# A row block transposed by DMA instead of TensorE in a fused matrix product and RMS norm, and loads moved behind transposes

## The chip, the core and the metric

One core of one Trainium2 chip. The metric is device microseconds of one execution, as the median of three runs. A profiled execution has its own time, the program's span and a little around it.

## The reference

```python
x = np.matmul(a, b)                 # a, b: 2048 x 2048, float32
rms = np.sqrt(np.mean(x ** 2, axis=-1, keepdims=True) + eps)
return (gamma * x / rms).astype(np.float32)
```

## The kernel before

The 16 row blocks of `a` (128 rows each) are multiplied with `b`, which lies in SBUF as bf16 (`raw[j][kp]`, left or right half of the columns j, a pair of 128-row tiles kp). Two scratch memories matter: SBUF tiles and eight PSUM banks, `tbank` and `acc[0]` to `acc[6]`, each 128 x 512 f32. The schedule is manual: every engine works through its instructions in the order in which the code lists them, and semaphores order the engines against each other. An engine that waits holds back all that is listed behind it on the same engine. The same is true of POOL's and SP's DMA issues.

**Head (blocks 0 to 3).** While `b` streams in, TensorE transposes these blocks into `head_at` and forms their left half plainly, then the right half of blocks 0 and 1 plainly (`stream_right`, banks `plain` = `acc[0]` to `acc[3]`). The right half of blocks 2 and 3 (`PAIR`) goes by a seven-product scheme (Strassen-Winograd): two blocks by two halves of K, and sums of quarters of `a` and of `b` in place of an eighth product. Its banks are `u2` = `acc[4]`, `u4` = `acc[5]`, `p7` = `acc[6]`. `b_diff` and `b_rest` build the sums of `b` on DVE.

**Groups (blocks 4 to 15).** Group g holds blocks 2g and 2g+1, g = 2 to 7; a half n is a group and a column half j. `do(n, m)` issues product m of half n, eight matmuls of 128 x 128 by 128 x 512, into its bank, and for m = 1, 6, 7 an ACT copy of that bank. `take(n, ..)` brings a result chunk from PSUM to its x tile on ACT or adds it on DVE. `a_sums(g, which)` builds on DVE the sums of quarters of `a` that products 3, 5, 6 and 7 load as weights: sum 2 for product 6, sum 3 for product 7, sum 4 for product 3; product 5 uses sum 1. Groups 4 and 5, and 6 and 7, share a second level of the scheme (`step`, `b_two`, `a_two_sums`, `block_segment`, `last_group`).

**A block's way in.** `load_block(mb)` puts a 1 MB load on POOL's DMA queue; the tile comes from a pool of two, except block 8's, which lies in the second half of `head_flat`. `wait_for(x)` is a one-element copy on POOL, which holds every later load until x is there. `row_norm(mb)` is two squares and a root on ACT, `row_factor` four tiny DVE operations that make a power of two, and DVE scales the block to fp16. Blocks 6 and later go through `prepare`: two scaled halves (`a16_half` and the block's own memory), each transposed by a DMA on SP's queue (`dma_start_transpose`) into `at_even` or `at_odd`. Blocks 4 and 5 are scaled whole (`row_apply`, lines 244 to 246) and transposed on TensorE (`transpose_half`, line 198), eight 128 x 128 transposes per half, into `tbank` and another bank, and copied from there (`take_transposed`, line 205).

**A block's way out.** `square_half` and `square_right` (ACT) sum the squares and take the root, `take_pre` adds parts on DVE, `finish(mb, ..)` takes the reciprocal and scales each half on DVE and stores it from SP. A slot of `x_slot` serves several blocks, so a later `take` waits for the store before.

Around the change the order before is, at the top level (lines 519 to 558): the pair's product 7, product 6 into `u2`, the DVE copy `u4` <- `u2` (line 529), scaling of blocks 4 and 5, product 3 into `acc[0]`, product 5 into `u4`, the transposes of block 4, product 4 into `u2` with the two halves of block 5's transposes (`turn`) inside and behind it, `load_block(8)`, and block 5's sums. Then `first_segment` runs half 0, and `segment(n)` the rest. Inside `segment(n)`, product 3 of the half before and product 1 of the half behind are listed among the half's own. Half n = 0 runs 1, 7, 2, 6, half 1's product 1, then 5 and 4.

Of the kernel before, what the change touches and what calls it, by code (L numbers as in the profile page):

```python
# [17 lines left out]
def kernel(  # L18
# [13 lines left out]
    nc = tc.nc  # L32
# [215 lines left out]
    def prepare(mb):  # L248
        row_factor(mb)
        src, f = a32.pop(mb), factor.pop(mb)  # L250
        for h, dst in enumerate((a16_half, src.bitcast(FP16)[:, 0:HALF])):
            nc.vector.tensor_scalar_mul(out=dst, in0=src[:, h * HALF:(h + 1) * HALF], scalar1=f)
            nc.sync.dma_start_transpose(at(mb)[:, h * KP:(h + 1) * KP, :], dst)
# [222 lines left out]
    def stream_right(kp):  # L476
# [11 lines left out]
        if kp == KP - 1:  # L488
            product_matmul(PAIR, 1, 7, p7, kp - 1, True)
        product_matmul(PAIR, 1, 2, u4, kp, True)  # L490
# [4 lines left out]

    for kp in range(KP):
# [22 lines left out]
    r2, r3 = HB - 2, HB - 1  # L519
    x11, x12, x21, x22 = (x_chunk(r, c) for r in (r2, r3) for c in (2, 3))  # L520
    copy_on("A")(out=x11, in_=u2)
# [6 lines left out]
    product(PAIR, 1, 6, u2, start=False)  # L528
# [5 lines left out]
    row_apply(HB + 1)  # L534
    evict(plain[2:3], "A")
    product(PAIR, 1, 3, acc[0])
    product(PAIR, 1, 5, u4, start=False)
    turned = [transpose_half(HB, h, (tbank, acc[1])[h]) for h in range(2)]
    take_transposed(HB, 0, turned[0], nc.scalar.copy)
    take_transposed(HB, 1, turned[1], nc.vector.tensor_copy)  # L540
    load_block(HB + 3)
    for r in range(HB):
        take_pre(r)
    square_right(0)
    evict(plain[3:], "A")
    square_right(1)

    def turn(h):
        view = transpose_half(HB + 1, h, (tbank, acc[2])[h])
        take_transposed(HB + 1, h, view, nc.vector.tensor_copy)  # L550

    for kp in range(KP):
        if kp == 6:
            turn(0)
        product_matmul(PAIR, 1, 4, u2, kp, False)
    turn(1)
    load_block(HB + 4)
    a_sums(G0, (3, 1, 2), False)

    def pair_ends():  # L560
        nc.scalar.copy(out=x22, in_=p7)
        nc.scalar.copy(out=x12, in_=u4)
        add(x21, u2, x22)
        add(x22, x12, x22)
        add(x12, acc[0], x12)
# [4 lines left out]
    B1, B2, B3, B7 = (acc[1], acc[0]), acc[3:5], (acc[6], acc[5]), acc[2]  # L570

# [4 lines left out]
    def do(n, m, copies=True):  # L576
# [4 lines left out]
        b1, b2, b3 = B1[n % 2], B2[n % 2], B3[n % 2]  # L581
# [13 lines left out]
    def take(n, what, engine="A"):  # L595

        x11, x12, x21, x22 = chunks(n)
        if what == 11:
            copy_on(engine)(out=x11, in_=B1[n % 2])
# [11 lines left out]
    def first_segment():  # L611
        n, g, j = 0, G0, 0
        nxt = 2 * g + 2
        do(n, 1)
        do(n, 7, False)
        finish(0, (1,))
        pair_ends()
        do(n, 2)
        row_norm(nxt)
        a_sums(g, (4,))  # L620
        finish(0, (0,))
        do(n, 6)
        do(n + 1, 1)
        prepare(nxt)
# [287 lines left out]
```

## Time and profile before

| | |
|---|---|
| median of 3 runs | 219.05 us (219.04 to 219.17) |
| profiled execution | 218.97 us |
| its span | 217.2 us |
| granted TensorE clock | 0.995 |
| TensorE busy | 207.3 us, 95% |
| VectorE busy | 161.4 us, 74% |
| ScalarE busy | 113.1 us, 52% |
| GpSimd busy | 35.6 us, 16% |
| DMA moved | 46.60 MB, mean 215 GB/s |

Rows of the timeline give the start in us, the duration, the engine, the line, the operation with the tile written and read, and the shape; rows that follow each other are merged with a count. In brackets stands the idle time of that engine before the row and what ended it. A row "SPq" or "POOL DMA" is the issue of a DMA, not the transfer. Durations of neighbouring rows of one engine overlap a little, since they are pipelined.

### The profile page before, as it was taken

To read this page: it belongs to the slowest core of one execution; us is meant where nothing else is said; L and a number is where in the kernel's file an instruction comes from. 1 tells how busy PE (TensorE), PEld (TensorE's weight loads), DVE (VectorE), ACT (ScalarE), POOL (GpSimd) and SP (SyncE) were. 2 spreads that over 40 slices of the span, in tenths; PEclk is the share of its full clock that TensorE was granted. 3 is DMA by queue.
4 is the path that set the end of the run, shared out by engine and by line. 5 is a ranking of instruction groups with operands and counts; after the bars stand their busy time and mean duration, and the time that the engine had idled before them with its cause. 6 is when DMAs were issued, how large, how long until landed. Compare 5 with 4: busy or idle time off the path is not lost.

```text
span 217.2 us, 2953 instructions
## 1 busy us (share of the span) xinstructions
PE 207.3 (95%) x1000; PEld 97.2 (45%) x1020; DVE 161.4 (74%) x323; ACT 113.1 (52%) x222; POOL 35.6 (16%) x74
## 2 busy tenths in 40 slices
PE   7999999999999999999999999999999999999960
PEld 3544544444455444444444444444444444444420
DVE  1128869999899997788975899399859883385771
ACT  2110002900599569498626962585777651555771
POOL 7554444334001000100021001102010000000020
PEclk9999999999999999999999999999999999999997
DMA  7999999999959798978674975499985960040455
GB/s 152 168 202 210 201 204 210 212 206 213 405 202 382 290 263 229 330 295 241 162 239 172 340 246 96 187 237 271 278 307 153 284 218 0 0 193 3 193 191 195
DMA packets 37040, 46.60 MB, mean 215 GB/s; under 512 B 22561, under 2 KB 26657, under 8 KB 35745
## 3 DMA queue, kind: packets, MB, share of 16 engines
q0 software_dynamic: 10608, 23.86, 44.8%
q1 hardware_dynamic: 26144, 22.29, 33.9%
q10 hardware_dynamic: 272, 0.26, 0.3%
q8 instruction: 8, 0.13, 0.2%
q14 instruction: 8, 0.06, 0.1%
HBM read 34.60 MB, written 16.78 MB: 237 GB/s over the span
## 4 chain that ended last, share of the span: by engine, by line
PE 68%; DMA 23%; DVE 2%; POOL 2%; issue 2%; ACT 1%; ACTq 0%; DVEq 0%; POOLq 0%
PE acc L361 61%; DMA b<-in_b_dram 18%; DMA early<-in_a_dram 5%; PE acc L400 3%; PE tbank L400 2%; POOL b L115 1%; DVE early L101 1%; PE tbank L361 1%; POOL early L119 1%; ACT a L779 1%; PE acc L198 0%; PE tbank L198 0%; DVE acc L529 0%; DVE x L101 0%; DVE b L101 0%
## 5 line engine op out<-in xcount | busy, mean ns | idle before, releaser
L361 PEld LDWEIGHTS <-s 128*128 128x128 f16 (+1 forms) x312 | 30.5, 98 | 36.9 <-DVE s L338 0.3
L275 ACT ACTIVATE sq<-x 128x1024 bf16<-128x1024 f32 (+1 forms) x33 | 33.2, 1005 | 22.6 <-DVE x L101 18.8
L409 PE MATMUL acc<-b,head_at 128*128 128x512 bf16 x171 | 42.1, 379 | 0.2
L314 DVE SCALAR_TENSOR_TENSOR x<-x,r,gamma_sb 128x1024 f32<-128x1024 f32 x28 | 35.0, 1282 | 0.5
L361 PE MATMUL acc<-b,head_at 128*128 128x512 bf16 x135 | 33.9, 379 | 0.2
L101 DVE TENSOR_TENSOR x<-acc,x 128x512 f32<-128x512 f32 x33 | 22.2, 686 | 12.5 <-PE acc L361 6.7
L361 PEld LDWEIGHTS <-head_at 128*128 128x128 f16 (+1 forms) x192 | 18.7, 98 | 22.2
L361 PE MATMUL acc<-b,at_even 128*128 128x512 bf16 x110 | 26.2, 379 | 0.1
L361 PE MATMUL acc<-early,s 128*128 128x512 bf16 x100 | 25.3, 379 | 0.2
L409 PEld LDWEIGHTS <-head_at 128*128 128x128 bf16 x176 | 16.9, 98 | 19.1
L361 PE MATMUL acc<-b,s 128*128 128x512 bf16 x102 | 24.1, 379 | 0.2
L227 ACT ACTIVATE sq<-a 128x1024 bf16<-128x1024 f32 x22 | 23.3, 1058 | 1.7 <-DMA a<-in_a_dram 1.4
L361 PEld LDWEIGHTS <-at_even 128*128 128x128 f16 x160 | 15.6, 98 | 18.6
L361 PE MATMUL acc<-t_left,s 128*128 128x512 bf16 x93 | 22.2, 379 | 0.1
L115 POOL DMA_DIRECT2D b<-in_b_dram x32 | 17.2, 540 | 20.5 <-DMA b<-in_b_dram 13.8
L448 ACT COPY x<-acc 128x512 f32<-128x512 f32 x7 | 4.0, 581 | 25.3 <-PE acc L409 25.3
L591 ACT COPY acc<-acc 128x512 f32<-128x512 f32 x12 | 6.9, 575 | 10.4 <-PE acc L361 10.4
L190 DVE COPY head_at<-tbank 128x1024 bf16<-128x1024 bf16 x7 | 4.8, 693 | 7.5 <-PE tbank L185 7.5
L296 DVE RECIPROCAL r<-rms 128x1 f32<-128x1 f32 x16 | 2.5, 159 | 9.7 <-ACT rms L291 9.7
L101 DVE TENSOR_TENSOR x<-tbank,x 128x512 f32<-128x512 f32 x9 | 6.2, 690 | 4.2 <-PE tbank L438 4.1
L782 POOL TENSOR_SCALAR x<-x,r 128x512 f32<-128x512 f32 x2 | 1.4, 688 | 47.8 <-DVE r L296 47.8
L593 ACT COPY x<-acc 128x512 f32<-128x512 f32 x10 | 5.8, 584 | 5.3 <-PE acc L361 4.9
(129 smaller groups left out, 243.4 us busy)
## 6 DMA issues: line engine op xcount, KB each, us to landing
out_dram<-x SPq DMA_DIRECT2D x29, 512.0 KB, 3.0
a<-in_a_dram POOLq DMA_DIRECT2D x9, 1024.0 KB, 6.0
b<-in_b_dram POOLq DMA_DIRECT2D x32, 256.0 KB, 9.9
a<-in_a_dram POOLq DMA_DIRECT2D x4, 512.0 KB, 9.8
early<-in_a_dram POOLq DMA_DIRECT2D x7, 256.0 KB, 10.0
gamma_sb<-in_gamma_dram POOLq DMA_DIRECT2D x2, 512.0 KB, 9.8
head_at<-in_a_dram POOLq DMA_DIRECT2D x1, 1024.0 KB, 7.8
out_dram<-x SPq DMA_DIRECT2D x3, 256.0 KB, 2.6
```

Of the source, the lines that this page charges most:

```text
L101: nc.vector.tensor_tensor(out=out, in0=in0, in1=in1, op=op)
L115: nc.gpsimd.dma_start(out=raw[j][kp][:, t, :], in_=b[lo:lo + P, j * HALF:(j + 1) * HALF])
L190: nc.vector.tensor_copy(out=head_at[:, 2 * kp:2 * kp + 2, :, :], in_=view)
L227: nc.scalar.activation(out=junk, in_=a32[mb][:, h * HALF:(h + 1) * HALF], func=ACTF.Square, scale=2.0 ** -8, accum_out=n2[:, h:h + 1])
L275: nc.scalar.activation(out=sq[:, 0:src.shape[-1]], in_=src, func=ACTF.Square, scale=inv_sqrt_n, accum_out=msq[mb][:, c:c + 1])
L314: nc.vector.scalar_tensor_tensor(out=x, in0=x, scalar=inverse_of[mb], in1=gamma_sb[:, h * HALF:(h + 1) * HALF], op0=ALU.mult, op1=ALU.mult)
L361: nc.tensor.matmul(bank, lhsT[:, kp, :], rhs, start=(start and kp == 0), stop=(kp == KP - 1), skip_group_check=not start)
L400: nc.tensor.matmul(bank, lhsT[:, k, :], rhs, start=(m in (1, 7) and k == 0), stop=(k == KQ - 1), skip_group_check=m not in (1, 7))
L409: nc.tensor.matmul(bank, head_at[:, kt, r, :], head_rhs(c, kt), start=(kt == 0), stop=(kt == KT - 1))
L448: copy_on(engine)(out=x_chunk(*g), in_=banks[g])
L591: nc.scalar.copy(out=b3, in_=b2)
L593: nc.scalar.copy(out=chunks(n)[2], in_=B7)
```

## The change

Block 5 is scaled in two halves into `a16_first` and transposed by two DMAs from SP's queue. Its TensorE transposes and their two DVE copies are gone. The pair's products are reordered: four matmuls of product 6 are listed inside the last `stream_right`, product 3 is split into 4, 2 and 2 matmuls, product 5 stands before product 4, and block 4's transposes come after six matmuls of product 4. Evictions of the pair and of `plain` are moved. Half 0 and half 1 now start with products 1 and 2 of both halves, half 1's product 1 going to `tbank`; then the rest of product 3, and half 0's product 7. Product 6 of half 1 is listed in `first_segment`. Block 7's load waits on POOL for block 6's landing. Block 8's load is listed behind block 7's transposes, block 9's behind block 8's landing, block 10's behind block 8's transposes, block 11's behind block 9's transposes. The norms and scalings of blocks 10, 11, 12 and 13 are each listed one place earlier; block 12's transposes are listed apart from its scaling, behind the second-level product 2.

```diff
--- before.py
+++ after.py
@@ -245,12 +245,19 @@
         a16[mb] = a16_slot[mb]
         nc.vector.tensor_scalar_mul(out=a16[mb], in0=a32.pop(mb), scalar1=factor.pop(mb))
 
-    def prepare(mb):
+    to_turn = {}
+
+    def prepare(mb, turn=True):
         row_factor(mb)
         src, f = a32.pop(mb), factor.pop(mb)
-        for h, dst in enumerate((a16_half, src.bitcast(FP16)[:, 0:HALF])):
+        to_turn[mb] = a16_half, src.bitcast(FP16)[:, 0:HALF]
+        for h, dst in enumerate(to_turn[mb]):
             nc.vector.tensor_scalar_mul(out=dst, in0=src[:, h * HALF:(h + 1) * HALF], scalar1=f)
-            nc.sync.dma_start_transpose(at(mb)[:, h * KP:(h + 1) * KP, :], dst)
+            if turn:
+                turn_half(mb, h)
+
+    def turn_half(mb, h):
+        nc.sync.dma_start_transpose(at(mb)[:, h * KP:(h + 1) * KP, :], to_turn[mb][h])
 
     x_half = {}
     slot_of = {(r, h): r + HB * h for r in range(HB) for h in range(2)}
@@ -486,13 +493,18 @@
         for g, kt in first:
             head_matmul(banks[g], *g, kt)
         if kp == KP - 1:
+            copy_on("A")(out=x11, in_=u2)
             product_matmul(PAIR, 1, 7, p7, kp - 1, True)
+            for k in range(4):
+                product_matmul(PAIR, 1, 6, u2, k, False)
         product_matmul(PAIR, 1, 2, u4, kp, True)
         if kp < KP - 1:
             product_matmul(PAIR, 1, 7, p7, kp - 1, True)
         for g, kt in second:
             head_matmul(banks[g], *g, kt)
 
+    r2, r3 = HB - 2, HB - 1
+    x11, x12, x21, x22 = (x_chunk(r, c) for r in (r2, r3) for c in (2, 3))
     for kp in range(KP):
         load_later(1)
         b_diff(1, kp)
@@ -516,58 +528,56 @@
 
 
 
-    r2, r3 = HB - 2, HB - 1
-    x11, x12, x21, x22 = (x_chunk(r, c) for r in (r2, r3) for c in (2, 3))
-    copy_on("A")(out=x11, in_=u2)
     product_matmul(PAIR, 1, 7, p7, KP - 1, True)
     b_rest(1, KP - 1)
     add(x11, u4, x11)
     evict(plain[:1], "A")
     row_norm(HB)
     row_norm(HB + 1)
-    product(PAIR, 1, 6, u2, start=False)
+    for kp in range(4, KP):
+        product_matmul(PAIR, 1, 6, u2, kp, False)
     nc.vector.tensor_copy(out=u4, in_=u2)
     row_factor(HB)
     row_apply(HB)
     evict(plain[1:2], "D")
     row_factor(HB + 1)
-    row_apply(HB + 1)
-    evict(plain[2:3], "A")
-    product(PAIR, 1, 3, acc[0])
-    product(PAIR, 1, 5, u4, start=False)
+
+    def part(m, bank, lo, hi, start=False):
+        for kp in range(lo, hi):
+            product_matmul(PAIR, 1, m, bank, kp, start)
+
+    part(3, acc[0], 0, 4, True)
+    part(5, u4, 0, KP)
+    part(4, u2, 0, 6)
     turned = [transpose_half(HB, h, (tbank, acc[1])[h]) for h in range(2)]
     take_transposed(HB, 0, turned[0], nc.scalar.copy)
     take_transposed(HB, 1, turned[1], nc.vector.tensor_copy)
+    src, f = a32.pop(HB + 1), factor.pop(HB + 1)
+    for h in range(2):
+        half = slice(h * HALF, (h + 1) * HALF)
+        nc.vector.tensor_scalar_mul(out=a16_first[:, half], in0=src[:, half], scalar1=f)
+        nc.sync.dma_start_transpose(at(HB + 1)[:, h * KP:(h + 1) * KP, :], a16_first[:, half])
+    wait_for(a32[HB + 2][:, 0:1])
     load_block(HB + 3)
     for r in range(HB):
         take_pre(r)
-    square_right(0)
+    part(4, u2, 6, KP)
+    part(3, acc[0], 4, 6, True)
+    nc.scalar.copy(out=x21, in_=p7)
+    nc.scalar.copy(out=x12, in_=u4)
     evict(plain[3:], "A")
-    square_right(1)
-
-    def turn(h):
-        view = transpose_half(HB + 1, h, (tbank, acc[2])[h])
-        take_transposed(HB + 1, h, view, nc.vector.tensor_copy)
-
-    for kp in range(KP):
-        if kp == 6:
-            turn(0)
-        product_matmul(PAIR, 1, 4, u2, kp, False)
-    turn(1)
-    load_block(HB + 4)
-    a_sums(G0, (3, 1, 2), False)
-
-    def pair_ends():
-        nc.scalar.copy(out=x22, in_=p7)
-        nc.scalar.copy(out=x12, in_=u4)
-        add(x21, u2, x22)
-        add(x22, x12, x22)
-        add(x12, acc[0], x12)
+    add(x22, x12, x21)
+    add(x21, u2, x21)
+    evict(plain[2:3], "D")
+    x12_pair = x12
 
 
 
     halves = [(g, j) for g in range(G0, NG) for j in range(2)]
     B1, B2, B3, B7 = (acc[1], acc[0]), acc[3:5], (acc[6], acc[5]), acc[2]
+
+    def b1_of(n):
+        return tbank if n == 1 else B1[n % 2]
 
     def chunks(n):
         g, j = halves[n]
@@ -578,7 +588,7 @@
         if n >= len(halves) or n < 0:
             return
         g, j = halves[n]
-        b1, b2, b3 = B1[n % 2], B2[n % 2], B3[n % 2]
+        b1, b2, b3 = b1_of(n), B2[n % 2], B3[n % 2]
         if g >= G2:
             b1 = b2
         product(g, j, m, {1: b1, 2: b1, 3: b3, 4: b2, 5: b3, 6: b2, 7: B7}[m],
@@ -596,7 +606,7 @@
 
         x11, x12, x21, x22 = chunks(n)
         if what == 11:
-            copy_on(engine)(out=x11, in_=B1[n % 2])
+            copy_on(engine)(out=x11, in_=b1_of(n))
         elif what == 12:
             copy_on(engine)(out=x12, in_=B3[n % 2])
         elif what == 22:
@@ -612,25 +622,34 @@
         n, g, j = 0, G0, 0
         nxt = 2 * g + 2
         do(n, 1)
+        square_right(0)
+        do(n + 1, 1)
+        square_right(1)
+        do(n, 2)
+        do(n + 1, 2)
+        part(3, acc[0], 6, KP, True)
+        finish(0, (1,))
+        a_sums(g, (3, 1, 2), False)
         do(n, 7, False)
-        finish(0, (1,))
-        pair_ends()
-        do(n, 2)
         row_norm(nxt)
-        a_sums(g, (4,))
+        prepare(nxt)
+        add(x12_pair, acc[0], x12_pair)
         finish(0, (0,))
         do(n, 6)
-        do(n + 1, 1)
-        prepare(nxt)
+        product(g, 1, 6, B2[1], False)
         do(n, 5)
         nc.scalar.copy(out=chunks(n)[2], in_=B7)
+        finish(1, (0,))
+        a_sums(g, (4,))
         take(n, 22)
         row_norm(nxt + 1)
+        nc.scalar.copy(out=B3[1], in_=B2[1])
         take(n, 11)
-        finish(1)
+        square_right(r2)
+        prepare(nxt + 1)
         do(n, 4)
         take(n, 21)
-        prepare(nxt + 1)
+        finish(1, (1,))
         square_half(2 * g + 1, j)
 
     X2, W2, Y2 = tbank, B1[1], B1[0]
@@ -647,20 +666,21 @@
             block_segment(n)
             return
         first = g >= G2 and (g - G2) % 2 == 0
-        do(n, 6)
-        own = nxt + (g == NG - 2)
+        if n > 1:
+            do(n, 6)
+        own = nxt + (g >= G2)
         if j == 0:
             finish(ra - 1)
             row_norm(own)
-        elif g == G0:
-            square_right(r2)
         do(n - 1, 3)
         take(n - 1, 12)
         if j == 0:
             square_right(ra - 2)
             prepare(own)
+            if g == G2 - 1:
+                load_after(at(nxt)[:, KT - 1, 0:1], nxt + 2)
             a_sums(g, (4,))
-            finish(ra - 2, (0, 1) if g < NG - 2 else (0,))
+            finish(ra - 2, (0, 1) if g < G2 else (0,))
         else:
             if not first:
                 square_half(ra, 0)
@@ -673,16 +693,18 @@
                 b_two(4)
             elif not first and g > G2:
                 finish(ra - 2)
-        if g < G2:
+        if g < G2 and n > 1:
             do(n, 2)
             take(n, 11)
         if g == G2 - 1 and j == 1:
             b_two(3)
             b_two(1)
         do(n + 1, 1)
+        if n == 1:
+            take(n, 11)
         if j == 1 and g + 2 < NG:
             wait_for(at(nxt + 1)[:, KT - 1, 0:1])
-            if G0 < g < NG - 3:
+            if g in (G0, G2):
                 load_block(nxt + 2)
                 wait_for(a32[nxt + 2][:, 0:1])
             load_block(nxt + 3)
@@ -691,15 +713,15 @@
                 a_two_sums(g)
             a_sums(g + 1, (1, 2))
         do(n, 7)
-        if j == 0 and g < NG - 2:
+        if j == 0 and g < G2:
             row_norm(nxt + 1)
         if j == 1:
             a_sums(g + 1, (3,))
-            if g == NG - 3:
+            if G0 < g < NG - 2:
                 row_norm(nxt + 2)
         do(n, 5)
         take(n, 22)
-        if j == 0 and g == NG - 2:
+        if j == 0 and g >= G2:
             finish(ra - 2, (1,))
         if j == 1:
             take_pre(rb)
@@ -709,13 +731,13 @@
         take(n, 21)
         if j == 0:
             square_half(rb, 0)
-            if g < NG - 2:
+            if g < G2:
                 prepare(nxt + 1)
             if g == G2:
                 b_two(2)
         else:
-            if g == NG - 3:
-                prepare(nxt + 2)
+            if G0 < g < NG - 2:
+                prepare(nxt + 2, g != G2)
             if not first:
                 square_right(rb)
             if g == G0:
@@ -728,14 +750,15 @@
         do(n, 6)
         step(g - 1, 1, X2)
         nc.scalar.copy(out=W2, in_=X2)
-        row_norm(nxt)
+        row_norm(nxt + 1)
         do(n - 1, 3)
         step(g - 1, 2, W2)
+        for h in range(2):
+            turn_half(nxt, h)
         step(g - 1, 6, X2)
         nc.scalar.copy(out=Y2, in_=X2)
         square_right(ra - 1)
         add(x00, W2, x00)
-        prepare(nxt)
         load_after(at(nxt)[:, KT - 1, 0:1], nxt + 2)
         do(n + 1, 1)
         take(n - 1, 12)
@@ -745,14 +768,13 @@
         step(g - 1, 7, W2)
         step(g - 1, 4, X2)
         add(x11, Y2, x11)
-        row_norm(nxt + 1)
         add(x10, W2, x10)
         add(x11, W2, x11)
         take_pre(ra - 2)
+        prepare(nxt + 1)
         do(n, 7)
         add(x10, X2, x10)
         a_sums(g, (4,))
-        prepare(nxt + 1)
         step(g - 1, 3, Y2)
         do(n, 5)
         take(n, 22)
```

## The prediction

> **What bounds the kernel.** I read the page's totals and slices first, then the chain that ended last, then the timelines of single engines around the edit, where the next stall is decided.
>
> ```profile
> PE 207.3 (95%) x1000; PEld 97.2 (45%) x1020; DVE 161.4 (74%) x323; ACT 113.1 (52%) x222; POOL 35.6 (16%) x74
> PE   7999999999999999999999999999999999999960
> PE 68%; DMA 23%; DVE 2%; POOL 2%; issue 2%; ACT 1%; ACTq 0%; DVEq 0%; POOLq 0%
> ```
>
> TensorE is full in every slice but the first and the tail. No other engine sets the pace; each only has to hand over in time.
>
> The chain in order of time, where the edit lies:
>
> ```profile
> 63.35 0.45 PE tbank L198 x8
> 63.80 0.45 PE acc L198 x8
> 64.25 1.29 PE acc L361 x6
> 65.54 0.45 PE tbank L198 x8
> 65.99 0.43 PE acc L361 x2
> 66.42 0.45 PE acc L198 x8
> ...
> 67.14 10.74 PE acc L361 x49
> ```
>
> These are matmuls and transposes back to back: 49 matmuls and one 0.05 gap in 10.79 us, so 0.216 a matmul, 1.727 a product of eight; eight transposes take 0.45. From here to 210.2 the chain is almost all TensorE. So time is won only by what TensorE no longer does and lost only where it is made to wait.
>
> Three timelines decide the waits (DVE's, the SP queue's, POOL's):
>
> ```profile
> 60.02 0.70 DVE L529 COPY acc<-acc 128x512 f32<-128x512 f32 x1
> 61.33 1.28 DVE L246 TENSOR_SCALAR x<-a,s 128x2048 f16<-128x2048 f32 x1
> 65.01 0.68 DVE L205 COPY at_even<-acc 128x1024 f16<-128x1024 f16 x1
> ```
> ```profile
> 82.62 1.24 SPq L253 DMA_TRANSPOSE head_at<-a_half  x1
> 84.03 1.24 SPq L253 DMA_TRANSPOSE head_at<-a  x1
> ...
> 151.33 1.24 SPq L253 DMA_TRANSPOSE at_even<-a_half  x1
> 152.74 3.21 SPq L253 DMA_TRANSPOSE at_even<-a  x1
> ```
> ```profile
> 63.15 0.53 POOL L137 DMA_DIRECT2D a<-in_a_dram  x1 [8.56 <-ACT norm L230]
> 87.23 0.18 POOL L146 CAST pace<-head_at 128x1 f32<-128x1 f16 x1 [19.98 <-DMA head_at<-a]
> 149.93 0.53 POOL L137 DMA_DIRECT2D a<-in_a_dram  x1
> 158.11 0.18 POOL L146 CAST pace<-at_even 128x1 f32<-128x1 f16 x1 [7.65 <-DMA at_even<-a]
> ```
>
> A second half issued alone at 84.03 wakes POOL at 87.23: 3.2 us. One issued at 152.74, behind the 1 MB load of 149.93, wakes it at 158.11: 5.4 us. The load goes first. That is the danger of the change.
>
> **Removed from TensorE.** Block 5's 16 transposes, 65.54 and 66.42: 2 x 0.45 = **0.90 us**. Products are moved, none dropped. Also gone: two DVE copies of 0.69.
>
> **The reordered pair products.** Four matmuls of product 6 move ahead of P2's last. They need the ACT copy of u2, 55.84 to 56.43, and TensorE gets there at 56.72: free. They push the second heads, and with them the ACT eviction of 57.35 and block 4's norms, back by 4 x 0.216 = 0.86. Product 3 is cut into 4 + 2 + 2, so product 5 is reached 0.86 earlier, at 60.60 instead of 61.47. It writes u4, which DVE copies until 60.02 + 0.70 = 60.72. That copy waits for product 6, which still ends at 59.9. With 0.06 for the handover (an addition on DVE ends at 68.32, the weight load that it releases starts at 68.38): 60.80, a **stall of 0.20**, nothing in between. Then eight of product 5 and six of product 4: block 4's transposes at 60.80 + 14 x 0.216 = 63.82. Block 4's scaling moved from 61.33 to 62.15 and ends at 63.43: 0.3 in hand. The second half (64.27) writes the bank whose eviction moved from 62.52 to 63.34 and ends at 64.02: 0.2 in hand. Transposes end at 64.72; four more matmuls to 65.58. Block 4's first product then needs the DVE copy that frees its bank. That starts when the transposes are through (64.88) and takes 0.68: 65.61. **Stall of about 0.10**, start at 65.68. Before it was 66.70, with 0.43 of product 3 then done already: net gain so far 66.70 - 65.68 - 0.43 = 0.59.
>
> **Block 5 by DMA.** DVE scales two halves from 65.55; the form with 1024 columns takes 0.74 (at 75.70), so 66.28 and 67.07. Two more DMAs go on SP's queue, where nothing waits ahead; the next behind them is the first store. Issue at 66.36 and 1.44 later (as 76.52 and 77.96), 67.80. Alone the pair lands at 71.0 (3.2). Block 6's load now waits for the later scaling: issue 64.0 to 64.3 for 63.15. Its landing is bounded by the loads' 5.0 least to 7.8 most; the nearest is its own, whose last packet in the trace is 4.3 after the issue (67.5). So its data pass until 68.4 and the transposes follow until about 71.1, landed 71.4; behind a load as at 149.93, 73.2; at the worst of before (5.8), 73.6. I take 71.4, because the load starts 2.1 to 2.4 ahead of the first half and not 1.4 as there. What hides it: four products of block 4 and the last two of product 3, from 65.68 to 73.02. DVE is in the first store's scaling until 71.1 (the root ready at 69.6, 0.15 and 1.28 after it), then builds the sums for product 7 (0.69): 72.15, with **0.87 in hand**. Without that cover each us late is a us lost. The sums for product 6 are ready at 73.65, needed at 74.75.
>
> [...] The rows have 56 ns each in TensorE's stream (0.45 for eight) and 4.6 us for the pair of DMAs (82.62 to 87.23), and the sum goes by them.
>
> **Behind it.** Block 7's load waits on POOL for block 6's landing, 68.8, so it is issued at 69.4 and is at full rate only 2 us later: past the transposes. It lands near 74.3; its norms start at 77.65. Block 6's norm is ready at 74.1, its transposes issue at 75.75 (76.52 before). Then DVE's queue: prepare, addition, two stores' scalings, sums 4 at 79.8, the addition that frees product 3's bank until 81.25. TensorE is there at 81.65: 0.35 in hand, the tightest later place. Block 7's transposes issue at 82.7 and 84.1, land at 87.3, as before.
>
> **Block 8's load** moves from 66.72 to behind that landing: 87.9. The load at 87.82 in the trace of before, with the same stores beside it, has its last packet at 93.1; block 8's norms were at 93.70 and come to 93.55. So 0 to 0.5 us of ACT waits, hidden: block 8's first product is due near 107.5, its transposes at 98. Block 9's load follows at 94 and lands by 100.5 (its norms: 100.19 before); its sums have 2.5 us in hand at 114.5. Blocks 10, 11, 12 and 13 are normed and transposed earlier than before, one place each, in gaps of ACT (3.65 before 116.04, 4.65 before 137.75): priced at nothing; if those gaps were closed, 2.4 us of ACT each, still not on TensorE's path. Block 12's transposes wait for the last reader of their slot (about 140.5), 3 us sooner than their issue at 143.50.
>
> **Sum.** -0.90 + 0.20 + 0.10 = **-0.60**. The profiled execution took 218.97 (span 217.2 and 1.77 around it) and would take 218.37; the median stands 0.08 above it: 219.05 - 0.60 = **218.45**.
>
> **Rivals.**
>
> *Block 5 lands late* (slower). Place: the sums for product 7 on DVE, mechanism the load that passes first. It decides from a landing later than 72.3. At the worst of before, 73.6, the sums end at 74.35 and product 7 waits 1.35: 219.05 - 0.60 + 1.35 = 219.8. If block 7's load got in between as well, the landing would be 75.4 (that load's last packet at 69.4 + 4.3, and 1.7 for the half behind it) and the loss 3.1: 221.5. For: 5.4 and 5.8 were seen, and block 7's load waits for block 6's, not for these transposes. Against: here block 6's load is nearly through.
>
> [...]
>
> *Eaten by small waits* (no change). The 0.2 and 0.3 in hand at block 4's transposes and 0.35 at 81.65 all hang on ACT and DVE queues that moved by 0.86. If two of them are missed by 0.2 to 0.3, the gain is 0.1 to 0.2: 218.9.
>
> *No new stall at all*: the whole 0.90, 218.15. Against it: product 5 reaches u4's copy too early by the trace's own ends. It is the low end of my forecast, not a case apart.
>
> **Chances.** A measurement of this kernel can tell about 0.2%, 0.44 us, from no change. The forecast (218.15 to 218.6): 0.66. Small waits, 218.6 to 219.49: 0.17. Late transposes, above: 0.17. The forecast's gain is only 0.16 beyond what can be told. The range from 218.05 to 219.5 leaves out the late case.
>
> **What would show it.** Right: TensorE without rows of `a_first`, block 4's first product near 65.7, a DVE row for product 7's sums at 71.2 to 72.3, product 7 at 73.0, the chain's last matmul end near 209.6. Wrong: idle time of DVE's sums put down to a DMA into at_even, and TensorE waiting for them near 73; or TensorE idle near 81.65 behind the addition. A gain beyond 0.9 or a loss after 94 would mean that I misread what bounds it.

## The result, and the profile after

The change made the kernel slower: 222.33 us (221.30 to 224.15, 6 runs) against 219.07 us for the kernel before on the same chip; the ratio is 1.0151 [1.0128, 1.0174], some 3.3 us. The predicted 218.45 and its range were wrong, on the side to which I had given 0.17.

The profiled execution took 222.38 us, with a span of 220.6 us. The page has the busy totals, the 40 slices of TensorE and the shares of the last chain:

```profile
PE 207.5 (94%) x985; PEld 95.9 (43%) x1004; DVE 160.5 (73%) x323; ACT 112.2 (51%) x221; POOL 36.0 (16%) x76
...
PE   7999999999999999999999989989999999999960
...
PE 70%; DMA 12%; DVE 7%; ACT 4%; issue 3%; POOL 1%; DVEq 0%; ACTq 0%; POOLq 0%
```

No engine has noticeably more work than before. Two slices, from 126.8 to 132.4 and from 143 to 149, roughly, fall from 9 to 8, and DVE and ACT now hold 7% and 4% of the chain. So it is waits, and they lie far behind the edit in the pair's products. Taking each interval from one matmul's start to the next in the trace and subtracting the regular 0.216 (0.056 for a transpose), I find no wait over 0.06 us in the kernel before and these in the kernel after (an interval of two regular steps, which comes about once in 50 matmuls, is taken as a matmul whose record is missing: the profile of before counts 1020 weight loads for 1000 matmuls): 0.16 at 61.0, 0.08 at 65.8, 0.50 at 73.7, 0.61 at 115.7, 1.21 at 129.0 (and 0.07 at 130.8), 0.70 at 146.2, 0.40 at 150.9. That is 3.73; with the 0.90 won, 2.8. The last matmul starts 3.06 later (212.86 for 209.80), and the 0.2 that is left stands ahead of the edit, since ACT's copy of `u2` already starts at 56.05 for 55.84; the tail behind the last matmul gives 0.3 more, which makes the span's 3.4. (The idle times in the rows below are shorter, because the profile counts them from a matmul's modelled end.)

**At 73.** The timeline of the kernel after (rows of POOL, SP, DVE and PE):

```profile
64.12 0.53 POOL L137 DMA_DIRECT2D a<-in_a_dram  x1 [9.34 <-ACT norm L230]
...
66.47 4.33 SPq L559 DMA_TRANSPOSE at_even<-a_first  x2
...
72.92 0.69 DVE L345 TENSOR_TENSOR s<-at_even 128x1024 f16<-128x1024 f16 x1 [1.64 <-DMA at_even<-a_first]
...
73.67 1.68 PE L368 MATMUL acc<-t_left,s 128*128 128x512 bf16 x7 [0.34 <-DVE s L345]
```

The chain in order of time, all TensorE here before, now goes through it:

```profile
67.85 4.97 DMA at_even<-a_first
...
72.92 0.70 DVE s L345
...
73.67 7.73 PE acc L368 x35
```

DVE waited 1.64 us for block 5's tiles and TensorE for DVE: block 5 came late, as my first rival had it, but it cost 0.5 us only.

**From 88 to 116.** Block 8's and 9's loads, the squares of their norms, block 10's load, block 9's transposes, and the product that waits:

```profile
88.25 0.53 POOL L137 DMA_DIRECT2D head_at<-in_a_dram  x1
...
95.41 1.06 ACT L227 ACTIVATE sq<-head_at 128x1024 bf16<-128x1024 f32 x1 [1.51 <-DMA head_at<-in_a_dram]
...
96.11 0.53 POOL L137 DMA_DIRECT2D a<-in_a_dram  x1
...
103.73 1.06 ACT L227 ACTIVATE sq<-a 128x1024 bf16<-128x1024 f32 x1 [2.21 <-DMA a<-in_a_dram]
...
106.31 0.53 POOL L137 DMA_DIRECT2D a<-in_a_dram  x1 [0.37 <-ACT sq L227]
...
107.93 1.24 SPq L260 DMA_TRANSPOSE at_even<-a_half  x1
...
109.33 3.02 SPq L260 DMA_TRANSPOSE at_even<-a  x1
...
114.28 0.70 POOL L146 CAST pace<-at_even 128x1 f32<-128x1 f16 x1 [7.45 <-DMA at_even<-a]
...
115.73 1.47 PE L368 MATMUL acc<-t_left,s 128*128 128x512 bf16 x6 [0.45 <-DVE s L345]
```

Each load waits on POOL for what stands before it, so each lateness is handed on. Block 10's load was let go by block 8's transposes and got ahead of block 9's, which were seen 4.95 us behind the issue of their second half. In the kernel before, block 10's load comes behind block 9's transposes, and these are seen 3.26 us behind their issue:

```profile
106.68 1.25 SPq L253 DMA_TRANSPOSE at_even<-a  x1
...
109.94 0.71 POOL L146 CAST pace<-at_even 128x1 f32<-128x1 f16 x1 [21.59 <-DMA at_even<-a]
```

So block 9's tiles come 4.34 later than before: 2.65 because they are issued later, and 1.69 because they take longer, behind block 10's load.

**Near 128.**

```profile
124.85 0.75 DVE L255 TENSOR_SCALAR a_half<-a,s 128x1024 f16<-128x1024 f32 x1 [0.70 <-DMA head_at<-a_half]
...
128.30 0.68 DVE L101 TENSOR_TENSOR x<-acc,x 128x512 f32<-128x512 f32 x1
...
129.04 1.24 PE L368 MATMUL acc<-b,s 128*128 128x512 bf16 x5 [1.05 <-DVE x L101]
```

Block 11's scaling writes `a16_half`, which block 10's transposes still read: DVE waits 0.70, and the addition that frees TensorE's bank stands behind the scaling.

**Near 144 and 150.**

```profile
137.62 0.53 POOL L137 DMA_DIRECT2D a<-in_a_dram  x1 [0.34 <-DVE s L345]
...
143.01 1.06 ACT L227 ACTIVATE sq<-a 128x1024 bf16<-128x1024 f32 x1 [1.92 <-DMA a<-in_a_dram]
...
145.57 0.58 ACT L759 COPY acc<-tbank 128x512 f32<-128x512 f32 x1
...
146.20 1.02 PE L407 MATMUL acc<-b,x 128*128 128x512 bf16 x4 [0.53 <-ACT acc L759]
...
147.79 2.48 DVE L321 SCALAR_TENSOR_TENSOR x<-x,r,gamma_sb 128x1024 f32<-128x1024 f32 x2
...
150.92 1.02 PE L407 MATMUL acc<-b,x 128*128 128x512 bf16 x4 [0.24 <-DVE x L101]
```

ACT stands 1.92 us at block 13's norm, which the change lists one place earlier, and behind it stands the copy of line 759 that the second level's next product needs. A root behind that copy releases a `finish` late, whose 2.48 us of scaling then stand ahead of the addition for 150.92.

### The profile page after: what moved, and what is told of

Read it like the earlier page. It is cut to its first block, busy times and chain, and to the rows that moved or that the text cites. A ratio compares the mean times of both kernels' runs of the same rounds, so it can differ in the third digit from the quotient of the medians.

```text
span 220.6 us, 2927 instructions
## 1 busy us (share of the span) xinstructions
PE 207.5 (94%) x985; PEld 95.9 (43%) x1004; DVE 160.5 (73%) x323; ACT 112.2 (51%) x221; POOL 36.0 (16%) x76
## 4 chain that ended last, share of the span: by engine, by line
PE 70%; DMA 12%; DVE 7%; ACT 4%; issue 3%; POOL 1%; DVEq 0%; ACTq 0%; POOLq 0%
PE acc L368 46%; PE acc L416 16%; DMA early<-in_a_dram 3%; PE acc L407 3%; DMA a<-in_a_dram 2%; DMA at_even<-a_first 2%; DMA at_even<-a 2%; DMA head_at<-a_half 2%; ACT sq L227 2%; DVE x L101 2%; PE tbank L445 2%; PE tbank L185 2%; DVE s L345 2%; PE tbank L407 1%; PE tbank L368 1%
## 5 line engine op out<-in xcount | busy, mean ns | idle before, releaser
L368 PE MATMUL acc<-b,s 128*128 128x512 bf16 x104 | 24.7, 379 | 1.0 <-DVE x L101 1.0
L368 PE MATMUL acc<-b,at_even 128*128 128x512 bf16 x93 | 22.4, 379 | 0.1
L455 ACT COPY x<-acc 128x512 f32<-128x512 f32 x6 | 3.4, 592 | 26.1 <-PE acc L416 26.1
L603 ACT COPY x<-acc 128x512 f32<-128x512 f32 x10 | 5.9, 586 | 9.1 <-DMA out_dram<-x 4.7
L601 ACT COPY acc<-acc 128x512 f32<-128x512 f32 x11 | 6.3, 575 | 7.8 <-PE acc L368 7.8
```

Of the source, the lines that this page charges most:

```text
L368: nc.tensor.matmul(bank, lhsT[:, kp, :], rhs, start=(start and kp == 0), stop=(kp == KP - 1), skip_group_check=not start)
L601: nc.scalar.copy(out=b3, in_=b2)
L603: nc.scalar.copy(out=chunks(n)[2], in_=B7)
```

## The experiments

In every kernel of this section, the two copies included, each transposing DMA is replaced by a plain DMA of the same half tile from the same queue, in 256 B pieces; those tiles are therefore not transposed. They fill every second place of the block instead of eight places in a row, which matters only at the end of this section. Times are medians; "before" measured between 218.95 and 219.26 beside them. "Waits" are TensorE's, counted as above. My theory after reading the trace: the late block 8 and the waits it feeds behind 110 cost more than the front wins. The rival: the front itself (block 5, the pair's order) is what loses.

### Do the copies stand for the kernels?

The copy of the kernel before, and of the kernel after:

```diff
-            nc.sync.dma_start_transpose(at(mb)[:, h * KP:(h + 1) * KP, :], dst)
+            nc.sync.dma_start(out=at(mb)[:, h::2, :], in_=dst.rearrange("p (t m) -> p t m", m=P))
```

> The kernel before with each transposing DMA replaced by a plain DMA of the same tile half on the same queue, in pieces of 256 B, tiles not transposed (so its products are of other numbers; nothing else is left out). It is the base for the copies of the changed kernel. If TensorE sets the pace and the pairs land within 5 us as the transposes did, 219.0 (218.8 to 219.5) with no gap on TensorE over 0.25 us. If the plain pieces are much slower, over 220.

> The changed kernel with the same replacement. Late-chain theory (block 8's late load makes every later load, norm and turned tile late, and what was moved one place earlier waits for it): the gaps of the changed kernel return, 221 to 223, with waits near 115, 129, 146 and 151 us. [...]

Measured: the copy of before 219.01, ratio 0.9994 [0.9979, 1.0009], no wait; the copy of the change 220.89, ratio 1.0083 [1.0055, 1.0111], with 1.15 at 127.7, 0.19 at 144.4, 0.41 at 149.1, 0.10 at 114.5, and none at 73. The copy loses 1.9 us of the 3.3. It serves for the later waits; the rest is taken up at the end.

### Front or rest?

Four kernels split the copy of the change. *Rest alone*: the front of before (block 5 on TensorE, the old order) with block 8's late load and the earlier places of blocks 10 to 13. *Front alone*: the front of the change, with block 8's load right behind block 7's and all else as before. *Block 8 early*: the copy of the change with only that load moved up. *Block 8 late, no moves*: the front and the late block 8, with blocks 10 to 13 in their places of before. The edits, cut to their core:

```diff
 # block 8 early, and front alone
     load_block(HB + 3)
+    load_block(HB + 4)
...
-            if g in (G0, G2):
+            if g == G2:                # block 8 early
+            if G0 < g < NG - 3:        # front alone, as before
+            if G0 <= g < NG - 3:       # block 8 late, no moves (without the load_block above)
 # front alone, and block 8 late without moves: places of before
-        own = nxt + (g >= G2)
+        own = nxt + (g == NG - 2)
...
-        row_norm(nxt + 1)
+        row_norm(nxt)
```

> The front of before with the late load of block 8 and the earlier norms of blocks 10 to 13; plain DMAs. Late-chain theory: 219.0 plus the gaps that the changed kernel has after 80 us in this form (1.15 and 0.41, and small ones), 220.5 to 221.8. Moves theory: the same. Front theory: 219.3 or less.

> Plain DMAs of 256 B pieces in place of the transposing ones, as in both bases (219.01 with the order of before, 220.89 with that of the change). The changed front alone: block 8 loaded right behind block 7, blocks 10 to 13 normed, scaled and loaded where they were before. Late-chain theory (block 8's late load makes each later load and norm late): 0.90 less 0.3 at block 4, so 218.4 (218.1 to 218.8), no gap on TensorE over 0.25 us. Front theory (the front disturbs all that follows): 220.5 or more. Moves theory (norming a block one place earlier costs by itself): 218.4 too.

> The changed kernel with plain DMAs and one thing undone: block 8 is loaded right behind block 7, block 9 behind block 7's tiles as before; the norms of blocks 10 to 13 stay one place earlier. Late-chain theory: the gaps near 128 and 149 us go, 218.4 to 218.8. Moves theory: they stay, 220.5 to 221.2. Front theory: 220.5 or more.

> The changed front and block 8 loaded behind block 7's tiles with block 9 behind it, but blocks 10 to 13 normed, scaled and loaded where they were; plain DMAs. Late-chain theory: block 9 comes late, but no later load stands ahead of its tiles and nothing waits one place too early: 218.4 to 219.2. Moves theory: 218.4. If the late block 8 costs by itself: 220 or more.

Rest alone: 221.79, ratio 1.0124 [1.0109, 1.0139], with 1.33 at 116.2, 0.52 at 128.8, 0.34 and 0.41 near 146 and 150. So the rival falls: the loss is there without the front, and with it the kernel is 0.90 faster (220.89), though not by the transposes alone, since the waits differ too.

Front alone: 219.91, ratio 1.0046 [1.0029, 1.0063], a miss. It has no wait behind 92, as the theory wants, but a new one of 0.79 at 84.1, which the timeline of this kernel explains:

```profile
70.46 0.53 POOL L137 DMA_DIRECT2D head_at<-in_a_dram  x1
...
71.12 0.35 SPq L327 DMA_DIRECT2D out_dram<-x  x1
...
79.87 0.58 ACT L645 COPY x<-acc 128x512 f32<-128x512 f32 x1 [2.73 <-DMA out_dram<-x]
...
84.06 1.89 PE L371 MATMUL acc<-b,head_at 128*128 128x512 bf16 x8 [0.62 <-ACT x L613]
```

Block 7's load was issued at 69.94, block 8's at 70.46. The first store, issued at 71.12, freed its slot only 8.7 us later, and ACT waited for it; block 7's norm and the copy that TensorE needs stand behind it on ACT. With two loads back to back in its way, the early place of block 8 is no free repair.

Block 8 early: 220.97, ratio 1.0083 [1.0054, 1.0111], a miss by its time, because the same store (9.4 us here) costs 0.38 and 1.11 near 82 and 85. But its waits answer the question: the 1.15 near 128 is down to 0.09, while 0.48 and 0.41 stay near 145 and 150. The two regions have different causes.

Block 8 late, no moves: 222.09 (219.58 to 222.59), ratio 1.0116 [1.0058, 1.0173], the other way round than I expected. The profiled run was the 219.58, so this is the same kernel once more, for a second profile:

> Once more the changed front with block 8 behind block 7's tiles and blocks 10 to 13 where they were, plain DMAs, for a second profile: its runs gave 219.58 and 222.0 to 222.6. Late-chain theory: in the longer ones block 9's tiles or the loads behind them come later, with gaps on TensorE past 110 us that the profiled one had not; 222.

221.53 (2 runs), ratio 1.0118 [1.0098, 1.0139]: the late block 8 costs more without the earlier places than with them. From this kernel's timeline:

```profile
127.22 1.06 ACT L227 ACTIVATE sq<-a 128x1024 bf16<-128x1024 f32 x1 [4.18 <-DMA a<-in_a_dram]
...
132.29 0.60 SPq L249 DMA_DIRECT2D head_at<-a  x1
...
137.12 0.69 DVE L348 TENSOR_TENSOR s<-head_at 128x1024 f16<-128x1024 f16 x1
...
137.87 1.47 PE L371 MATMUL acc<-t_left,s 128*128 128x512 bf16 x6 [1.57 <-DVE s L348]
```

Block 11 itself is late here: loaded at 118.44, its norms start at 127.22, and TensorE waits 1.74 for its sums, besides 0.92 at 129.2 for block 10's tiles. So the earlier places are no idle reshuffling: they make up for part of the late block 8. In the profile of the 219.58 the same load was issued at 117.72 and took 7.6 us instead of 8.8, so that the norms start at 125.36 and TensorE waits 0.55; why the load was faster in this one of six executions stays open.

### Three repairs, one by one

Block 13's norms and scaling back where they were before; block 8 loaded behind block 6's tiles and block 9 behind block 7's; and block 11's first half scaled into a memory that nothing reads then:

```diff
 # norm of 13 back
-        row_norm(nxt + 1)
         do(n - 1, 3)
...
         add(x11, Y2, x11)
+        row_norm(nxt + 1)
...
-        prepare(nxt + 1)
         do(n, 7)
         add(x10, X2, x10)
         a_sums(g, (4,))
+        prepare(nxt + 1)
 # block 8 behind block 6 (first_segment)
         row_norm(nxt)
         prepare(nxt)
+        load_after(at(nxt)[:, KT - 1, 0:1], nxt + 2)
...
-            if g in (G0, G2):
+            if g == G2:
 # other memory for block 11
-        to_turn[mb] = a16_half, src.bitcast(FP16)[:, 0:HALF]
+        to_turn[mb] = a16_first[:, 0:HALF] if mb == 11 else a16_half, src.bitcast(FP16)[:, 0:HALF]
```

> The changed kernel with plain DMAs (220.89), one edit: the norms and the scaling of block 13 go back to their place of before, behind the first additions of the second level. Theory of the places (ACT waits for block 13's load and holds the copy that the second level's product 5 needs, and the root behind it holds DVE): the gaps near 144 and 149 (0.19 and 0.41) go, the one near 128 stays: 220.3 (220.0 to 220.6). Late-chain theory alone: a norm in its old place waits for the same load, 220.9.

> The changed kernel with plain DMAs (220.89), one edit: block 8 is loaded behind block 6's tiles, about 81 us, and not behind block 7's, about 87.5; block 9 follows block 7's tiles. Late-chain theory: block 8's and 9's tiles come 2 to 4 us earlier, block 9's before block 10's load, and the gaps near 128 and behind go or halve: 219.2 to 220.0. If the later places alone made the loss: 220.9.

> The changed kernel with plain DMAs (220.89), one edit: block 11's first half is scaled into a16_first, which is free then, and not into a16_half, so that DVE need not wait until block 10's half has been read from there. Theory that this wait near 124 makes the gap near 128: that gap (1.15) falls below 0.5, 220.0 (219.6 to 220.4). If DVE is late there for another reason (the norm of block 11): 220.9.

Norm of 13 back: 219.84, ratio 1.0043 [1.0028, 1.0058], 1.05 won (0.98 when each is taken against the kernel before beside it): the waits near 144 and 149 are gone, 1.01 stays at 127.4. Block 8 behind block 6: 220.32 (219.46 to 221.78), ratio 1.0066 [1.0036, 1.0096], outside what I expected: the wait near 128 is gone, 0.30 and 0.40 near 144 and 148 stay. Its median is the least certain of the three, with executions over 2.3 us. Other memory: 220.21, ratio 1.0060 [1.0045, 1.0075]: the wait near 128 goes from 1.15 to 0.42, the later two stay (0.45 and 0.41). The chain of this last kernel still shows the later cause:

```profile
136.05 5.04 DMA a<-in_a_dram
...
143.48 0.29 ACT norm L230
...
143.77 0.49 ACT acc L762
...
144.31 2.76 PE acc L410 x8
```

Load, norm, copy, TensorE. So each of the two regions yields to its own repairs and not to the other's.

### The repairs together

> The copy of the change, with block 8 loaded behind block 6's tiles, block 9 behind block 7's, and block 13's norms and scaling back in the place they had before. Theory (two separate losses, each with its own waits): the two repairs add. Block 8 behind block 6 gave 220.89 - 220.32 = 0.6, block 13's norms back 220.89 - 219.84 = 1.05, so 219.2 (219.0 to 219.5), with TensorE waiting neither near 128 nor near 144 and 149. Rival (one lateness that only shows in two places): the second repair finds nothing left to win, 219.8 to 220.3.

> The same with block 11's first half scaled into another tile besides. Theory: with block 8 behind block 6 the wait near 128 is gone already, so this adds nothing: the same 219.2 within 0.3. Rival (the tile is held too long whatever block 8 does): 218.5 to 218.9, below the kernel before.

The first two together: 219.58, ratio 1.0023 [1.0000, 1.0046]; all three: 219.52, ratio 1.0016 [1.0003, 1.0030]. The two repairs win 1.3 together, for 1.6 as a sum, just outside the range that I gave and below the rival's; the third adds nothing, as expected. The profiled run of the first took 218.96; its chain behind 72 is one piece of TensorE through all that had gone wrong:

```profile
71.11 1.73 PE tbank L371 x8
72.83 64.47 PE acc L371 x298
137.30 0.86 PE tbank L410 x4
```

Yet the median isn't below the kernel before: the profiled run is the second fastest of twelve, and what the others lose isn't in its trace. The profiled run of the second, 219.93, shows where the 0.9 won in front may go: TensorE waits 1.23 at 91.5, since block 8's load (81.07) now stands ahead of block 7's tiles (82.62 and 83.46), seen only at 90.02. That load took 7.1 us; in the profile of the first kernel it took 5.9 and the same wait is 0.14, so this place varies between executions of nearly the same kernel. So I put the front together with block 8 behind block 6, and blocks 10 to 13 in their places of before:

```diff
 # the kernel "block 8 late, no moves"
         prepare(nxt)
+        load_after(at(nxt)[:, KT - 1, 0:1], nxt + 2)
...
-            if G0 <= g < NG - 3:
+            if G0 < g < NG - 3:
```

> The front of the change, block 8 loaded behind block 6's tiles and block 9 behind block 7's, blocks 10 to 13 loaded, normed and turned in the places of before. Theory (the front wins 0.6; the loss lies in block 8's lateness and in the earlier norms): 218.4 to 219.2, TensorE without a wait behind 100. Rival (with block 8 there block 7's tiles land too late, as the 1.23 near 91 in the copy with all three repairs): a wait of 0.5 to 1.3 near 91 and 219.3 to 220.0.

219.22 against 219.26, ratio 1.0006 [0.9992, 1.0019]: no change. The wait is the rival's, and the time lies between the two ranges; the profiled run, 219.91, is one of the two longest of eleven. Its chain has one stop:

```profile
83.97 5.92 DMA head_at<-a
...
91.45 46.79 PE acc L371 x216
```

Block 7's second half is issued at 83.97 and lands 5.9 us later, behind block 8's load; TensorE waits 0.55 and then works on without a stop. No place that I tried for block 8's load costs nothing, and no version beat the kernel before.

### What of the other 1.4 us?

The change loses 3.3, its copy 1.9. I took block 5 for the cause, and made its tiles late in the copy by moving them in four DMAs: first in 128 B pieces, in the copy of the change and in the one with two repairs, then in 256 B pieces with block 7's load held until they had landed:

```diff
-        move(HB + 1, h, a16_first[:, half])
+        for q in range(2):      # 128 B pieces
+            cols = slice(q * P // 2, (q + 1) * P // 2)
+            nc.sync.dma_start(out=at(HB + 1)[:, h::2, cols],
+                              in_=a16_first[:, half].rearrange("p (t m) -> p t m", m=P)[:, :, cols])
 # instead: 256 B pieces, four tiles each
+            nc.sync.dma_start(out=at(HB + 1)[:, h + q * KP:(q + 1) * KP:2, :], in_=...)
...
-    wait_for(a32[HB + 2][:, 0:1])
+    wait_for(at(HB + 1)[:, KT - 1, 0:1])
```

> The copy of the change, with block 5's tiles moved in four DMAs of 128 B pieces instead of two of 256 B: two more issues of about 0.7 us on the SP queue, so they land 1.0 to 2.0 later, at 71.5 to 72.5, and block 7's load is issued as much later. Theory (block 5's late landing is what the transposing form adds): product 7 waits 0.1 to 0.9 near 73, the waits near 115 and 128 grow, and the time is 221.4 to 222.5 against 220.9 for the copy. Rival (the 1.4 us have to do with the later transposing DMAs alone): 220.7 to 221.3.

> The same four DMAs in the copy with block 8 behind block 6's tiles and block 13's norms in their old place (219.6). Theory: only product 7's own wait of 0.1 to 0.9 is added, nothing grows later: 219.7 to 220.5. Rival: the lateness of block 7's load comes back behind 110 here too, 220.6 to 221.5.

> The copy of the change, with block 5's tiles moved in four DMAs of four tiles each (256 B pieces, two more issues on the SP queue), and block 7's load held until the last of them has landed, not only until block 6's load has. They should land at 71.3 to 72.5 (70.5 in the copy, 72.3 in the change) and block 7's load be issued at 71.9 to 73.0 (70.3 and 72.2). Theory (what the change loses beyond its copy comes from this lateness): product 7 waits 0 to 0.7, waits come up near 115 and grow near 145, and the time is 221.4 to 222.5. Rival (it comes from the later transposing DMAs themselves): product 7's wait alone, 220.7 to 221.4.

> The same lateness in the copy with block 8 behind block 6's tiles and block 13's norms in their old place (219.6). Theory (the repairs leave room for it later): product 7's wait of 0 to 0.7 is added and nothing later, 219.6 to 220.4. Rival (the lateness finds a new wait behind 85): 220.5 to 221.5.

The small pieces overshot: DVE got its last tile at 77.1, not at 72, TensorE waited 3.92 us, and the times are 227.03, ratio 1.0368 [1.0339, 1.0396], and 224.82, ratio 1.0262 [1.0230, 1.0294]. They leave the question open, but show something else. The windows of the first one (us of the window; its length; busy us and instructions of PE, PEld, DVE, ACT and POOL; granted clock, DMA share, GB/s):

```profile
74.00:78.00 4.00, 0.85 (x4) 0.20 (x2) 0.84 (x2) 0.00 (x0) 0.00 (x0) 0.88 0.88 300
78.00:80.00 2.00, 1.40 (x4) 0.57 (x5) 1.80 (x6) 0.00 (x0) 0.00 (x0) 0.50 0.06 25
80.00:82.00 2.00, 2.00 (x7) 0.60 (x6) 1.99 (x3) 0.00 (x0) 0.00 (x0) 0.50 0.36 80
82.00:84.00 2.00, 2.00 (x6) 0.73 (x5) 1.96 (x4) 1.77 (x3) 0.00 (x0) 0.53 1.02 260
84.00:86.00 2.00, 2.00 (x11) 0.93 (x10) 0.55 (x1) 1.94 (x6) 0.00 (x0) 1.00 1.02 412
```

After the 3.92 us TensorE ran at half its clock for some 5 us (0.50 to 0.53 from 78 to 84), and the intervals between its matmuls there add up to 2.6 more than regular ones; the other waits are 3.6 longer than in the copy. Together that is the 6.1 us over the copy, to within 0.2.

The gentler pair made block 7's load late (73.04 and 73.45, for 70.28 in the copy), but not the tiles: their last packets are through at 71.7 in the first. The 70.5 that my expectation gives for the copy was read where fifteen sixteenths of the packets are through; the last is through at 71.95. So these two test the load alone. 221.03, ratio 1.0093 [1.0067, 1.0119], is in the rival's range and nothing against 220.89: block 7's tiles land at 86.7 all the same. With the repairs, 220.34, ratio 1.0048 [1.0031, 1.0065], is 0.8 above 219.58, with waits at 91.4 (0.92) and 128.2 (0.55): the time is in the theory's range, but the waits are the new ones that the rival named. This kernel's chain leads from the load of block 7 (73.45) through its norm and its tiles to the wait at 91.4; but waits there came in two kernels without the late load too (1.23 and 0.55), so how much of the 0.92 is its doing is not shown.

Then I saw what the copy makes easier. A sum reads every second place of a block. In the copy that is what one DMA fills; a transposing DMA fills eight places in a row, so that the first sum needs both. The last kernel gives the copy the places of the change, with the half's first tile read eight times as its source:

```diff
-        nc.sync.dma_start(out=at(mb)[:, h::2, :], in_=src.rearrange("p (t m) -> p t m", m=P))
+        nc.sync.dma_start(out=at(mb)[:, h * KP:(h + 1) * KP, :],
+                          in_=src[:, 0:P].unsqueeze(1).to_broadcast([P, KP, P]))
```

> The copy of the change, with each plain DMA filling the eight neighbouring places that the transposing one fills (its source is the half's first tile, read eight times), so that every sum needs both DMAs of a block, as in the change. Theory (a part of the open 1.4 us is that in the copy the first sum needs only the first DMA): the sums for product 7 come at 72.2 to 72.6 instead of 71.5, product 7 waits 0.1 to 0.5 near 73, the wait near 115 grows from 0.10 to 0.4 or more, and the time is 221.3 to 222.4 against 220.9. Rival (the form of the DMA itself, or later issues): 220.6 to 221.2, no wait at 73.

221.20 (220.86 to 221.57), ratio 1.0096 [1.0079, 1.0113]: at most 0.3 of the 1.4, at the upper end of the rival's range, and the interval still holds the copy's 1.0083. The wait near 115 grows to 0.38, almost as the theory has it; near 73 there is none:

```profile
72.52 0.69 DVE L349 TENSOR_TENSOR s<-at_even 128x1024 f16<-128x1024 f16 x1 [1.03 <-DMA at_even<-a_first]
```

The sum comes 1.0 later than in the copy, at 72.52, and is ready at 73.25, just in time: a wait of 0.50 at 61.2 in this one profile had pushed product 7 to 73.38. In the change it comes at 72.92. So in these two profiles the transposing DMAs are 0.4 later than plain ones in the same places (0.6 from the first issue, 66.47 and 66.68), and that turns a close call into the 0.50 at product 7. The later waits differ too (0.61 for 0.38 at 115.7, 1.21 for 0.83 at 129.0, 0.70 for 0.49 at 146.2), 0.82 together; the 0.50 at 61.2, for 0.16 in the change, takes 0.34 of it back. No run separates the form of the DMA from its timing there; that stays open.

## Why the prediction was wrong

**Right.** The removed transposes and the reordered products: waits of 0.16 and 0.08 for the 0.20 and 0.10 predicted, and block 4's first product at 65.83 for 65.68, in a trace that is 0.2 later from the start. In the kernel with two repairs the last matmul starts at 209.44, in the copy of before at 210.11: 0.67 earlier. Of this 0.17 stands ahead of the edit (ACT's copy of `u2` at 55.98 for 56.14); the other 0.50 is the 0.90 less 0.39 of waits, where the sum gave 0.60 with 0.30. The step of 0.216 a matmul is right, though not by the division that the prediction shows: its 10.79 us hold 49 rows and, with a missing record, 50 steps. The bank near 81.65, called the tightest later place, held.

**Block 5 by DMA: mis-sized.** The landing was taken as 71.4; DVE's sum began at 72.92. The price of lateness was right (each us behind 72.3 is one lost; 0.62 by that, 0.50 measured), so this term is 0.50 and not 0. In the packets the load's last one ends at 69.2, 0.8 later than I had it: the 4.3 that I took from the trace of before is where most of that load's packets end, and its last one ends 4.66 behind the issue (67.81). The transposing packets, of which the first start at 68.5, pause from 69.4 to 70.2; 19 of them take 1.5 to 1.97 us, where none of the plain ones takes over 0.06, and the second half is through at 72.3. Plain DMAs into the same places had the sum at 72.52, so 1.1 of the 1.5 us came without transposing too; why the plain ones are that late no run shows. Block 6's landing, put at 68.8, was seen on POOL only at 71.23, 2.0 behind the load's last packet (0.5 in the copy), so block 7's load was issued at 72.22 and not 69.4. In the copy a load of block 7 as late as 73.04 cost nothing that could be measured.

**Block 8's load: the step that failed.** "So 0 to 0.5 us of ACT waits, hidden" rests on a last packet at 93.1 for the load at 87.82. I had read where most of its packets end. The view of DMA issues in the trace of before, which the prediction did not use for that load, has (KB, us to landing):

```profile
a<-in_a_dram POOLq DMA_DIRECT2D x1, 1024.0 KB, 7.6
```

A last handful of its packets went one after another until 94.95. After, block 8's load took 7.1 in the same view and block 9's 7.6: norms at 95.41 for 93.55, and block 9 at 103.7 for 100.5. With block 9 3.2 late, and its transposes 1.69 longer behind block 10's load, which the prediction leaves out at this place, "2.5 us in hand at 114.5" became a wait of 0.61 at 115.7. In the copy, where that wait is 0.10, block 8 loaded behind block 6's tiles won some 0.6 and took away the wait near 128; that the 0.61 of the change would go with it is read from the trace and not shown by a run.

**Blocks 10 to 13 priced at nothing: the other step that failed.** I asked whether ACT had room for an earlier norm, and it had. I did not ask whether the block was there yet, and what stands behind the norm. Block 13's norm waited 1.92 for its load, and the copy of line 759 behind it was on TensorE's path: about 1.0 by the repair, the largest single part of the loss in the copy. Likewise block 11's scaling, moved earlier, met `a16_half` in use: 0.7 by the repair of the memory, though not beside the earlier block 8, which takes the same wait away. As a whole the four moves do not cost: without them the late block 8 cost more. Block 12's transposes issued at 141.18, near the 140.5 I had, and cost nothing that the waits show.

**The rivals.** Those that cost time were placed before 82, and the text says that a loss after 94 would mean a misreading of what bounds the kernel. It did: 2.99 of the 3.73 us of waits lie behind 100. The late transposes, the slower rival, had the right mechanism at product 7 at about a third of its price.

**Which goes first.** Of block 9's transposes, issued at 107.93 and 109.33, no packet starts before 111.34 in the trace of after; by then 120 of the 128 pieces of 8 KB of block 10's load, issued at 106.31, have started, and the last ends at 111.84. So the load went first again. At the pair that the prediction read, issued at 151.33 and 152.74 in the trace of before, the first packet starts at 155.26, and the load of 149.93 ends at 155.65. These rows settle the order; what makes the load go first they do not show.

## What to carry to other kernels

When a load is moved later, follow it down to the engine that waits: take its duration from the view of issues at that place (stores beside it included), pass the lateness on to every load that is gated behind it, and only then look for slack. When a step is listed earlier on an in-order engine, ask two things of it: is its input there at the new time, and what stands behind it in that queue. A schedule in which TensorE never stops can have several transfers that only just fit; a local gain of 0.4% was lost at five later places.

## What I had not expected of the hardware

A 512 KB store issued 0.7 us behind the second of two back-to-back 1 MB loads freed its slot after 8.7 us (9.4 in a second kernel); behind one load it took 6.4 and 6.5 in two others, and the stores' median from issue to landing was 3.0 in the window of before from 84 to 95. After a wait of 3.92 us TensorE's granted clock was 0.50 in the windows from 78 to 82, 0.53 from 82 to 84 and 1.00 from 84, and after one of 3.77 it was 0.50 from 80 to 82 in the repaired kernel, while after waits of up to 1.21 us it stayed at 1.00 in the windows (from 128 to 134 in the kernel after).
